# Products of a pair of heads in a fixed order, whole and one at a time

## The chip, the core and the metric

The kernel runs on one core of one Trainium2 chip. Its time is the device time of one launch in microseconds. The engines are named as in the profile: PE is TensorE (matmuls), PEld its weight loads, DVE is VectorE, ACT is ScalarE, POOL is GpSimd, SP is SyncE, which here only issues DMAs.

## The reference, cut to what matters

One decoder block on x of 512 tokens and width 2048, in float32. The part that the change touches projects x to the queries and to the gate of each head of the first attention:

```python
proj = h @ w_in[l]
(qa, kca, vca, ksa, vsa, kwa, vwa, za, ga,
 qb, kb, vb, zb) = jnp.split(proj, offsets, axis=-1)
qa = _rope(_heads(qa, N_HEADS_A, HEAD_DIM_A)).reshape(B, S, N_KV_A, GROUP_A, HEAD_DIM_A)
...
o_a = gates[..., 0:1] * o_cmp + gates[..., 1:2] * o_sel + gates[..., 2:3] * o_win
y_a = o_a.reshape(B, S, WIDTH_A) * jax.nn.silu(za)
```

There are eight heads of 128 (qa, za). After them come sixteen heads of 64 (qb, kb, vb, zb) with a sliding window, then the product with w_out, the residual and a final RMSNorm.

## The kernel before, in words

Every float32 operand of a matmul is split into two words, high and low, and a product takes three matmuls: high by high, low of one by high of the other, and high by low (`mm3`, L121 to L124). ACT makes the high word of a weight unit (128 x 1024) with a copy (L634), DVE the low word with a subtraction (L635). The pools hold three buffers for each word, so a unit that is split must wait until the third product before it has read its words.

The stage of interest is the loop over heads 1 to 7 of the first attention (L736 to L766). `pair(h)` projects the queries and the gate of one head together: the matrix of x and that of the weights are cut into quarters, and seven products of 128 x 256 outputs (Strassen's scheme in Winograd's form) replace eight. Each product is `prod` (L661): 8 x 3 = 24 matmuls with 256 moving columns each. They bear the names of their operands from x: "22", "p", "21", "12", "w", "u" and "q" in the order of the program. In the profile their lines are L122 to L124 with the tile pj; the operand is pu for "p" and "u", xh and xl for "22", "21", "12" and "w", and VH, VL, KH, KL for "q", which lies in buffers that are no longer needed for the second group of keys and values.

A head's four quarters of weights are loaded by SP into raw buffers (L671), raw0 to raw3, as x1 (quarter 3), x2 (quarter 0), x4 (quarter 2) and x3 (quarter 1). DVE forms the sums of quarters that the scheme needs in place (L684): x2 + x4, then x4 + x1, x2 + x1 and x2 + x3. The list `tags` says which buffer serves which quarter of the next head. The results of the products are combined into d and jj, by ACT copies (L700, L706, L712) and DVE additions (L684).

`attn_a(h)` (L534) is the attention of one head. For each of four blocks of 128 queries it makes a score tile (L557, tile sp, 3, 6, 6 and 9 matmuls), for which there is one PSUM buffer of three banks; DVE reduces it to minima while it scales it (L559, L563), ACT takes the exponentials (L569, L573) and scales them (L583, L585); PE transposes the weights (L595, L607, L609, tile tp), ACT and DVE split these again (L525, L526, L613 to L615), and PE multiplies with the values (L601 to L603, L616, L618, tile op).

The order in which the engines get their instructions is not written out by hand: a scheduler with a model of time picks, among instructions that are ready, and each engine then works its queue in that order. `tc.issue_after(x)` tells the scheduler to place an instruction behind x. In the kernel before, nothing binds the products of a pair to each other, so the scheduler may put matmuls of one product between those of another, and matmuls of attention of the head before between those of either.

After head 7 the even parts of x that the products' operands had replaced are loaded back (L642), two rope tables are loaded (L778, L779), and the second attention begins with the projection of its keys from two units of weights that were loaded ahead (L758 to L760). The buffers of these two units, and the counter `raws` from which later units take theirs, are set by hand.

Of the kernel before, what the change touches and what calls it, by code (L numbers as in the profile page):

```python
# [35 lines left out]
def hybrid_block(ctx, tc, xT, xtm, w0, w1s, w2s, wz, wq, wkb, wo0, wos, cw1, cw2, cpos, rope, tabs, sinks, gT, fg, out):  # L36
# [34 lines left out]
    last = {}  # L71

    raws = [0]

    def weights(tag):
        return (wk if tag == "raw3" else wp).tile([P, 1024], F32, name="raw", tag=tag, bufs=1)
# [5 lines left out]
    def words(place):  # L82
        return [wp.tile([P, 1088], F32R, name=nm, tag=nm)[:, place:place + 1024] for nm in ("whi", "wlo")]
# [35 lines left out]
    recent = {}  # L119

    def mm3(ps, ah, al, bh, bl, first, last, go_on=False):  # L121
        pe.matmul(ps, ah, bh, start=first, stop=False, skip_group_check=go_on)  # L122
        pe.matmul(ps, ah, bl, start=False, stop=False, skip_group_check=go_on)  # L123
        recent["mm"] = pe.matmul(ps, al, bh, start=False, stop=last, skip_group_check=go_on).ins  # L124
# [145 lines left out]
    H0, H1 = slice(0, 256), slice(256, 512)  # L270
# [115 lines left out]
    for g in range(2):  # L386
        act.activation(KH[g][:, 0:CMP], kct[:, g * 32:g * 32 + 32], AF.Copy)
        dve.tensor_tensor(out=KL[g][:, 0:CMP], in0=kct[:, g * 32:g * 32 + 32], in1=KH[g][:, 0:CMP].bitcast(F32),
                          op=ALU.subtract)
# [16 lines left out]
    def proj(src, parity=None, jobs=None, loaded=()):  # L406
        ps = psp.tile([P, S], F32, name="pj", tag="pj")
        ready = []
        ks = list(range(KT))
        if parity is not None:  # L410
            ks = list(range(parity, KT, 2)) + list(range(1 - parity, KT, 2))
        for i, k in enumerate(ks):
            while len(ready) < (2 if jobs or parity is not None or k >= 8 else 1):
                ready.append(load_unit(src[:, len(ready)], 1024,
                                       loaded=loaded[len(ready)] if loaded else None))
            if jobs and i in jobs:
                jobs[i]()
            hi, lo = ready[k // 8]
            js = slice((k % 8) * P, (k % 8) * P + P)
            mm3(ps, hi[:, js], lo[:, js], xh[:, k, :], xl[:, k, :], i == 0, i == KT - 1)  # L420
        return ps
# [42 lines left out]
    def z_evac(ps):  # L464
        zr = wk.tile([P, S], F32, name="zr", tag="t2", bufs=1)
        st = wk.tile([P, S], F32, name="st", tag="st")
        dve.tensor_tensor(out=zr, in0=ps, in1=rstdb, op=ALU.mult)
        act.activation(st, zr, AF.Tanh, scale=0.5)
        dve.scalar_tensor_tensor(out=st, in0=st, scalar=1.0, in1=zr, op0=ALU.add, op1=ALU.mult)
        return st  # L470
# [9 lines left out]
    def q_evac(ps, cos, sin):  # L480
        return q_split(q_rope(ps, cos, sin))

    def q_split(t1):
        qh = wk.tile([P, S], F32R, name="qh", tag="qh", bufs=1)
        ql = wk.tile([P, S], F32R, name="ql", tag="ql", bufs=1)
        act.activation(qh, t1, AF.Copy)
        dve.tensor_tensor(out=ql, in0=t1, in1=qh.bitcast(F32), op=ALU.subtract)
        return qh, ql
# [144 lines left out]
    def split(hi, lo, src):  # L633
        act.activation(hi, src, AF.Copy)  # L634
        last["lo"] = dve.tensor_tensor(out=lo, in0=src, in1=hi.bitcast(F32), op=ALU.subtract).ins  # L635
# [20 lines left out]
    def unit(raw):  # L656
        hi, lo = words(STILL)
        split(hi, lo, raw)
        return hi, lo

    def prod(bank, u, op, new):  # L661
        for m in range(8):
            cs = slice(m * P, m * P + P)
            ah, al = xf[op, m]
            mm3(bank, u[0][:, cs], u[1][:, cs], ah, al, new and m == 0, m == 7, not new)

    tags = ["raw0", "raw1", "raw2", "raw3"]

    def load_quarter(src, tag, quarter):
        t = weights(tag)  # L670
        last["dma"] = nc.sync.dma_start(t, src[quarter]).ins  # L671
        return t

    def pair(h, *early):
        src = wq[h - FIRST]
        early = list(early)
        c1, c2, c4, c3 = tags
        tags[:] = c4, c1, c3, c2

        def load(tag, quarter):  # L680
            return early.pop(0) if early else load_quarter(src, tag, quarter)

        def plus(out, a, b, op=ALU.add):
            return dve.tensor_tensor(out=out, in0=a, in1=b, op=op).ins  # L684

        pa, pb = [psp.tile([P, S], F32, name="pj", tag="pj") for e in range(2)]
        qv = wk.tile([P, S], F32, name="t1", tag="t1", bufs=1)
        zr = wk.tile([P, S], F32, name="zr", tag="xr", bufs=1)
        d, jj = qv[:, H1], zr[:, H0]
        x1 = load(c1, 3)  # L690
        u0 = unit(x1)
        x2 = load(c2, 0)
        u3 = unit(x2)
        x4 = load(c4, 2)
        with ExitStack() as behind:
            if "jj" in last:
                behind.enter_context(tc.issue_after(last["jj"]))
            plus(x2, x2, x4)
        prod(pb[:, H0], u0, "22", True)
        act.activation(d, pb[:, H0], AF.Copy, scale=-1.0)  # L700
        x3 = load(c3, 1)
        prod(pa[:, H0], u3, "p", True)
        plus(d, d, pa[:, H0])
        u2 = unit(x3)
        prod(pb[:, H0], u2, "21", False)
        act.activation(zr[:, H1], pb[:, H0], AF.Copy)  # L706
        plus(jj, d, zr[:, H1])
        u4 = unit(x2)
        plus(x4, x4, x1)
        plus(x2, x2, x1)  # L710
        prod(pa[:, H0], u4, "12", False)
        act.activation(qv[:, H0], pa[:, H0], AF.Copy)  # L712
        plus(jj, jj, qv[:, H0], ALU.subtract)
        u1 = unit(x4)
        prod(pa[:, H1], u1, "w", True)
        plus(d, d, pa[:, H1])
        u5 = unit(x2)
        plus(x2, x2, x3)
        prod(pb[:, H1], u5, "u", True)
        plus(d, d, pb[:, H1])  # L720
        t2 = wk.tile([P, S], F32, name="t2", tag="t2", bufs=1)
        for a, b in ((0, 64), (64, 0)):
            dve.tensor_tensor(out=t2[a:a + 64], in0=qv[b:b + 64], in1=sinA[b:b + 64], op=ALU.mult)
        dve.tensor_tensor(out=qv, in0=qv, in1=cosA, op=ALU.mult)
        dve.tensor_tensor(out=qv, in0=qv, in1=t2, op=ALU.add)
        qq = q_split(qv)
        u6 = unit(x2)
        prod(pb[:, H1], u6, "q", False)
        plus(jj, jj, pb[:, H1])
        last["jj"] = plus(zr, zr, rstdb, ALU.mult)  # L730
        st = wk.tile([P, S], F32, name="st", tag="st")
        act.activation(st, zr, AF.Tanh, scale=0.5)
        dve.scalar_tensor_tensor(out=st, in0=st, scalar=1.0, in1=zr, op0=ALU.add, op1=ALU.mult)
        return qq, st

    for h in range(8):  # L736
        if h < FIRST:
            qq = q_evac(q0, cosA, sinA)
            st = z_evac(proj(wz[8], 0))
            lows, highs = slice(0, 4), slice(4, 8)  # L740
            first = []
            with tc.issue_after(last["dma"]):
                first.append(load_quarter(wq[0], tags[0], 3))
                forms_back(0, lows)
                forms_back(1, lows)
            for c, quarter in zip(tags[1:], (0, 2, 1)):
                with tc.issue_after(last["dma"]):
                    first.append(load_quarter(wq[0], c, quarter))
            with tc.issue_after(last["dma"]):
                for f in (2, 3):  # L750
                    forms_back(f, lows)
                    forms_back(f, highs)
        else:
            qq, st = pair(h, *first) if h == FIRST else pair(h)
        if h == 7:
            early = []
            for u in range(2):
                early.append(weights(("raw3", "raw1")[u]))  # L758
                with tc.issue_after(last["dma"]):
                    last["dma"] = nc.sync.dma_start(early[u], wkb[:, u]).ins  # L760
        attn_a(h, *qq, st)
        if h == 3:
            for e in range(2):
                nc.sync.dma_start((KH, KL)[e][0].bitcast(F32), Kd[e])
            for e in range(2):
                nc.sync.dma_start((VH, VL)[e][:, 0].rearrange("p t w c -> p (t w c)").bitcast(F32), Vd[e])  # L766
# [133 lines left out]
        finish(8 + i, ob, st)  # L900

    kb1 = wk.tile([P, S], F32, name="kb1", tag="xr", bufs=1)
    raws[0] += 1
    q_rope(proj(wkb, parity=1, loaded=early), cosB, sinB, kb1)
    q2 = qb_evac(proj(wz[16]), 0)
    build_k(kb1, 0)
# [179 lines left out]
    for n in range(1, 4):  # L1086
# [51 lines left out]
        def plus(out, a, b, op=ALU.add):  # L1138
            dve.tensor_tensor(out=out, in0=a, in1=b, op=op)
# [52 lines left out]
        else:  # L1192
# [64 lines left out]
            u1 = [pair()]  # L1257
# [122 lines left out]
```

## Time and profile before

| | us |
|---|---|
| runs (3): median, lowest, highest | 820.22, 819.86, 821.95 |
| the profiled execution: time, span | 820.54, 818.8 |
| busy in the span: PE, DVE, ACT, POOL | 805.6, 666.6, 483.6, 67.7 |
| stage of heads 1 to 7 (196 to 401): PE, DVE busy of 205 | 203.17, 187.60 |

The profile is of one execution, whose own time stands beside its span. A matmul is recorded as busy from its start to a modelled end, and the next one starts before that end, so a start-to-start distance is the better measure of PE's pace; idle time in brackets behind a row is what is left after the modelled end of the one before, and after the arrow stands who ended it.

### The profile page before, as it was taken

How to read it: one execution, taken by the hardware profiler on the slowest of the kernel's cores; microseconds unless marked ns; L12 is line 12 of the kernel's file. 1: busy time of each engine (PE TensorE's matmuls, PEld its weight loads, DVE VectorE, ACT ScalarE, POOL GpSimd, SP SyncE). 2: the span in 40 equal slices, each digit the busy share in tenths (PEclk: the TensorE clock that was granted, in tenths of full speed). 3: DMA queues.
4: the chain of work that ended last, by engine and by line, in shares of the span. 5: the costliest groups of instructions: out<-in, count | busy, mean ns of one | idle time of the engine just before them, and what ended most of it. 6: DMA issues, size and time to landing. Idle time of an engine off the chain costs nothing.

```text
span 818.8 us, 14134 instructions
## 1 busy us (share of the span) xinstructions
PE 805.6 (98%) x5281; PEld 733.7 (90%) x5281; DVE 666.6 (81%) x1326; ACT 483.6 (59%) x1026; POOL 67.7 (8%) x54
## 2 busy tenths in 40 slices
PE   9999999999999999999999999999999999999996
PEld 8888898999999999999988888888888888999996
DVE  7859786966889899899876688887687799777895
ACT  6734456564867687786756365645444657543545
POOL 4500002020000000000011211011001000000000
PEclk9999999999999999999999999999999999999999
DMA  9665786898421322423742422222222257497845
GB/s 327 201 204 168 264 289 226 258 333 306 137 85 33 116 78 93 168 83 99 233 141 68 138 78 55 75 87 69 78 78 77 77 145 260 145 244 205 242 99 205
DMA packets 52116, 128.30 MB, mean 157 GB/s; under 512 B 4944, under 2 KB 17232, under 8 KB 52048
## 3 DMA queue, kind: packets, MB, share of 16 engines
q1 hardware_dynamic: 50032, 120.59, 43.9%
q0 software_dynamic: 1728, 6.29, 4.4%
q8 instruction: 41, 0.67, 0.3%
q10 hardware_dynamic: 288, 0.52, 0.2%
q14 instruction: 27, 0.22, 0.1%
HBM read 110.31 MB, written 17.07 MB: 156 GB/s over the span
## 4 chain that ended last, share of the span: by engine, by line
PE 85%; DVE 5%; DMA 4%; ACT 3%; issue 2%; POOL 1%; SPq 0%; DVEq 0%; ACTq 0%; POOLq 0%
PE pj L124 16%; PE pj L123 16%; PE pj L122 16%; PE bank L124 4%; PE bank L122 4%; PE oa L123 4%; PE bank L123 4%; PE oa L122 4%; PE oa L124 3%; PE sp L557 3%; DMA rw<-wos 2%; PE tp L595 2%; PE tp L879 2%; DMA xr<-xT 1%; PE spb L844 1%
## 5 line engine op out<-in xcount | busy, mean ns | idle before, releaser
L124 PE MATMUL pj<-xh,wlo 128*128 128x512 f32 (+1 forms) x560 | 194.9, 348 | 1.8 <-DVE wlo L635 1.8
L122 PE MATMUL pj<-xh,whi 128*128 128x512 f32 (+1 forms) x560 | 194.7, 348 | 0.0
L123 PE MATMUL pj<-xl,whi 128*128 128x512 f32 (+1 forms) x560 | 194.6, 347 | 0.0
L96 DVE TENSOR_TENSOR wlo<-raw,whi 128x1024 fp32r<-128x1024 f32 (+2 forms) x102 | 116.7, 1148 | 34.8 <-ACT whi L95 29.4
L95 ACT ACTIVATE whi<-raw 128x1024 fp32r<-128x1024 f32 (+1 forms) x101 | 95.0, 943 | 76.9 <-PE pj L123 22.8
L124 PEld LDWEIGHTS pj<-xh,wlo 128*128 128x128 f32 x560 | 105.4, 188 | 15.0 <-DVE wlo L635 2.4
L123 PEld LDWEIGHTS pj<-xl,whi 128*128 128x128 f32 x560 | 105.3, 188 | 13.1 <-issue 0.9
L122 PEld LDWEIGHTS pj<-xh,whi 128*128 128x128 f32 x560 | 105.3, 188 | 12.2
L635 DVE TENSOR_TENSOR wlo<-raw,whi 128x1024 fp32r<-128x1024 f32 x49 | 59.5, 1220 | 9.3 <-ACT whi L634 9.2
L634 ACT ACTIVATE whi<-raw 128x1024 fp32r<-128x1024 f32 x49 | 51.1, 1054 | 21.1 <-DVE raw L684 6.1
L123 PE MATMUL oa<-wlo,yh 128*128 128x256 f32 (+1 forms) x168 | 50.2, 299 | 0.1
L122 PE MATMUL oa<-whi,yh 128*128 128x256 f32 (+1 forms) x168 | 49.8, 298 | 0.6 <-ACT yh L954 0.6
L124 PE MATMUL oa<-whi,yl 128*128 128x256 f32 (+1 forms) x168 | 49.5, 298 | 0.0
L858 ACT ACTIVATE ttb<-ttb,sums 128x256 f32<-128x256 f32 (+1 forms) x64 | 30.1, 471 | 26.5 <-DVE sums L851 26.1
L525 ACT ACTIVATE ph<-tp 128x512 fp32r<-128x512 f32 x56 | 32.4, 592 | 14.9 <-PE tp L595 8.7
L123 PE MATMUL bank<-wlo,xh 128*128 128x256 f32 (+1 forms) x128 | 40.3, 317 | 0.3 <-DVE wlo L96 0.3
L124 PE MATMUL bank<-whi,xl 128*128 128x256 f32 (+1 forms) x128 | 39.9, 314 | 0.0
L526 DVE TENSOR_TENSOR pl<-tp,ph 128x512 fp32r<-128x512 f32 x56 | 37.8, 684 | 1.9 <-ACT ph L525 1.8
L122 PE MATMUL bank<-whi,xh 128*128 128x256 f32 (+1 forms) x128 | 36.7, 318 | 1.5 <-ACT whi L95 1.5
L122 PE MATMUL bank<-xh,whi 128*128 128x512 f32 x96 | 37.3, 400 | 0.0
L123 PE MATMUL bank<-xl,whi 128*128 128x512 f32 x96 | 36.9, 389 | 0.0
L573 ACT ACTIVATE tt<-tt,sums 128x128 f32<-128x128 f32 (+3 forms) x64 | 35.3, 554 | 1.2 <-DVE sums L563 1.2
(359 smaller groups left out, 2172.6 us busy)
## 6 DMA issues: line engine op xcount, KB each, us to landing
raw<-wz SPq DMA_DIRECT2D x36, 512.0 KB, 3.6
raw<-wq SPq DMA_DIRECT2D x28, 512.0 KB, 3.7
raw<-cw SPq DMA_DIRECT2D x16, 512.0 KB, 4.6
raw<-wos SPq DMA_DIRECT2D x12, 512.0 KB, 4.6
rw<-wos SPq DMA_DIRECT2D x10, 512.0 KB, 5.6
xr<-xT SPq DMA_DIRECT2D x16, 256.0 KB, 5.0
raw<-w SPq DMA_DIRECT2D x8, 512.0 KB, 4.5
fd<-ft SPq DMA_DIRECT2D x4, 1024.0 KB, 6.2
```

The lines of the kernel that those rows point to most:

```text
L95: last["hi"] = act.activation(hi[:, :width], rw[:, :width], AF.Copy).ins
L96: last["lo"] = dve.tensor_tensor(out=lo[:, :width], in0=rw[:, :width], in1=hi[:, :width].bitcast(F32), op=ALU.subtract).ins
L122: pe.matmul(ps, ah, bh, start=first, stop=False, skip_group_check=go_on)
L123: pe.matmul(ps, ah, bl, start=False, stop=False, skip_group_check=go_on)
L124: recent["mm"] = pe.matmul(ps, al, bh, start=False, stop=last, skip_group_check=go_on).ins
L525: act.activation(ph, tp, AF.Copy)
L526: dve.tensor_tensor(out=pl, in0=tp, in1=ph.bitcast(F32), op=ALU.subtract)
L557: pe.matmul(sp[:, a:b], qq[:, qs], kk[0][:, ko:ko + b - a], start=pi == 0, stop=pi == 2)
L573: act.activation(tv, tv, AF.Exp, bias=mn[:, i, 1 + w:2 + w], scale=-1.0, accum_out=dn[:, i, 1 + w:2 + w])
L634: act.activation(hi, src, AF.Copy)
L635: last["lo"] = dve.tensor_tensor(out=lo, in0=src, in1=hi.bitcast(F32), op=ALU.subtract).ins
L858: act.activation(tv, tv, AF.Exp, bias=mn[:, e, v:v + 1], scale=-1.0, accum_out=dn[:, e, v:v + 1])
```

## The change

Each product but "q" is recorded in `last["prod"]` by its last matmul, and the first matmul of every product of a pair is to be issued behind that one. "u" comes before "w" in the program, and with it unit u5 before u1; the addition x4 + x1 comes after "12". The buffers of the next head follow: its quarters x1, x2, x4 and x3 take the buffers that x1, x3, x4 and x2 had. The two early key units move to raw0 and raw3, and the counter of raw buffers goes on by two.

```diff
         for m in range(8):
             cs = slice(m * P, m * P + P)
             ah, al = xf[op, m]
-            mm3(bank, u[0][:, cs], u[1][:, cs], ah, al, new and m == 0, m == 7, not new)
+            with ExitStack() as behind:
+                if m == 0 and "prod" in last:
+                    behind.enter_context(tc.issue_after(last["prod"]))
+                mm3(bank, u[0][:, cs], u[1][:, cs], ah, al, new and m == 0, m == 7, not new)
+        if op != "q":
+            last["prod"] = recent["mm"]
...
         c1, c2, c4, c3 = tags
-        tags[:] = c4, c1, c3, c2
+        tags[:] = c1, c3, c4, c2
...
         u4 = unit(x2)
-        plus(x4, x4, x1)
         plus(x2, x2, x1)
         prod(pa[:, H0], u4, "12", False)
         act.activation(qv[:, H0], pa[:, H0], AF.Copy)
         plus(jj, jj, qv[:, H0], ALU.subtract)
-        u1 = unit(x4)
-        prod(pa[:, H1], u1, "w", True)
-        plus(d, d, pa[:, H1])
+        plus(x4, x4, x1)
         u5 = unit(x2)
         plus(x2, x2, x3)
         prod(pb[:, H1], u5, "u", True)
         plus(d, d, pb[:, H1])
+        u1 = unit(x4)
+        prod(pa[:, H1], u1, "w", True)
+        plus(d, d, pa[:, H1])
...
-                early.append(weights(("raw3", "raw1")[u]))
+                early.append(weights(("raw0", "raw3")[u]))
...
     kb1 = wk.tile([P, S], F32, name="kb1", tag="xr", bufs=1)
-    raws[0] += 1
+    raws[0] += 2
```

## The prediction

> **What bounds the kernel now.** I read the page first, then the busy times by stretch over the stage that the change touches (heads 1 to 7 of the first attention, 196 to 401 us), then who waited for whom there, then PE's timeline around each wait.
>
> ```profile
> span 818.8 us, 14134 instructions
> PE 805.6 (98%) x5281; PEld 733.7 (90%) x5281; DVE 666.6 (81%) x1326; ACT 483.6 (59%) x1026; POOL 67.7 (8%) x54
> PE 85%; DVE 5%; DMA 4%; ACT 3%; issue 2%; POOL 1%; SPq 0%; DVEq 0%; ACTq 0%; POOLq 0%
> ```
>
> ```profile
> 196.00:227.00 31.00, 30.68 (x249) 29.84 (x249) 28.35 (x64) 22.33 (x51) 0.00 (x0) 1.00 0.57 196
> 257.00:288.00 31.00, 31.00 (x255) 30.21 (x256) 28.47 (x63) 22.32 (x58) 0.00 (x0) 1.00 0.24 77
> 318.00:349.00 31.00, 30.04 (x251) 29.35 (x250) 27.43 (x62) 21.88 (x56) 0.00 (x0) 1.00 0.33 111
> sum 205.00, PE 203.17 PEld 198.59 DVE 187.60 ACT 152.11 POOL 0.00; mean PE 29.02 PEld 28.37 DVE 26.80 ACT 21.73 POOL 0.00
> ```
>
> PE is the bound. The last four lines are three of the seven stretches, one for each head, and their sum: PE is busy 203.17 of 205.00 us at a granted clock of 1.00, so its visible idle time in the whole stage is 1.83 us. DVE is second with 187.60, 92%, and it works in order, so it can hold PE up only where something that PE needs stands late in DVE's queue. Where that happens:
>
> ```profile
> PE pj L124 <- DVE wlo L635: 1.8, 3, 1.0
> ```
>
> ```profile
> 220.69 0.39 PE L124 MATMUL pj<-xh,wlo 128*128 128x256 f32 x1 [0.32 <-DVE wlo L635]
> 250.40 0.28 PE L123 MATMUL pj<-xl,whi 128*128 128x256 f32 x1
> 251.19 0.39 PE L124 MATMUL pj<-xh,wlo 128*128 128x256 f32 x1 [0.52 <-DVE wlo L635]
> 339.89 0.28 PE L123 MATMUL pj<-xl,whi 128*128 128x256 f32 x1
> 341.12 0.39 PE L124 MATMUL pj<-xh,wlo 128*128 128x256 f32 x1 [0.96 <-DVE wlo L635]
> ```
>
> Three waits are all there is. Each is the first matmul with the low word in the first product ("22") of the next head, after both matmuls that need only the high word. Why the low word is late shows in what PE did before the last of them:
>
> ```profile
> 331.02 0.28 PE L123 MATMUL pj<-pu,whi 128*128 128x256 f32 x1
> 332.22 0.28 PE L124 MATMUL pj<-pu,wlo 128*128 128x256 f32 x1
> 333.70 0.28 PE L122 MATMUL pj<-pu,whi 128*128 128x256 f32 x1
> 333.81 0.28 PE L122 MATMUL pj<-xh,whi 128*128 128x256 f32 x1
> ```
>
> Product "u" (operand pu) starts at 330.8, is broken off at 333.81 for the whole of "w" (operand xh), and ends only near 338.8. So its sum into d, and the weight words that it holds (three buffers for each word), come free late, and DVE meets the next head's split behind a score reduction. Such nesting is what the change forbids.
>
> **The change part by part.** *Order of the products.* Nothing is added or removed: the built order of the changed kernel has the same 5218 matmuls, and DVE's queue the same operations. Each product of a pair begins after the last matmul of the one before, and w comes after u. Attention may still cut in, and does: counted along PE's queue, the 49 products of the stage stand in 109 pieces before and in 107 after. What must go are nested products, and with them the causes of the three waits. From start to start the two large ones cost 341.12 - 339.89 - 0.11 = 1.12 and 251.19 - 250.40 - 0.11 = 0.68 us; with 0.32 for the small one that is 2.1 us. In the new order "q" is over before "22" of the next head begins, and DVE has that low word 1 to 4 us ahead of PE at all six borders between heads. What is late next is the chain of score tiles.
>
> That chain: the scores have one PSUM buffer (sp), so each of a head's four tiles waits until DVE has reduced the tile before, and DVE does it behind whatever stands ahead. Before, PE could fill such a time with a second product. To walk along the new order I need these prices:
>
> ```profile
> 293.14 0.18 DVE L559 CUSTOM_DVE_ANT_0 tc__3271<-sp,tab 128x32 f32<-128x32 f32 x1
> 293.94 2.35 DVE L635 TENSOR_TENSOR wlo<-raw,whi 128x1024 fp32r<-128x1024 f32 x2
> 385.07 2.35 DVE L635 TENSOR_TENSOR wlo<-raw,whi 128x1024 fp32r<-128x1024 f32 x2
> 387.34 1.28 DVE L526 TENSOR_TENSOR pl<-tp,ph 128x512 fp32r<-128x512 f32 x2
> 388.54 1.21 DVE L684 TENSOR_TENSOR raw<-raw 128x1024 f32<-128x1024 f32 x1
> 338.51 0.19 DVE L559 CUSTOM_DVE_ANT_0 tc__3674<-sp,tab 128x32 f32<-128x32 f32 x1 [1.36 <-PE sp L557]
> 339.85 1.22 DVE L635 TENSOR_TENSOR wlo<-raw,whi 128x1024 fp32r<-128x1024 f32 x1
> ```
>
> ```profile
> 262.03 0.74 PE sp L557 x6
> 295.35 1.08 PE sp L557 x6
> ```
>
> ```profile
> L634 ACT ACTIVATE whi<-raw 128x1024 fp32r<-128x1024 f32 x49 | 51.1, 1054 | 21.1 <-DVE raw L684 6.1
> raw<-wq SPq DMA_DIRECT2D x28, 512.0 KB, 3.7
> ```
>
> By starts, a split on DVE takes (387.34 - 385.07) / 2 = 1.14 us, and so does an addition of weights; a split of transposed scores 0.60; the reduction of the second score tile 293.94 - 293.14 = 0.80, of the fourth 339.85 - 338.51 = 1.34. The second and third tile take PE 0.74 and 1.08.
>
> The walk through head 4, from the end of "21" as zero. PE: "12" 24 x 0.117 = 2.8; two transposes 0.2; second score tile 0.74, to 3.75; six transposes 0.65, to 4.4; two matmuls of "u", to 4.65; then the third tile, which waits for the reduction of the second: DVE begins it at about 3.9 and ends it at 4.7, so PE loses 0.1 to 0.2. Third tile to 5.9. Next is u's first low word: DVE's split follows the reduction, 4.7 + 1.14 = 5.85, just in time. Later PE needs the buffer for the first tile of head 4's own scores at 26.1: DVE has reduced the fourth tile of head 3 at 26.1 to 26.3, and then come pcr and ql, each 0.1 behind PE. So 0.5 us for this head. Heads 5 and 7 show the same two places: about 0.4 (ql and pcr again), and about 0.2 (the first tile's reduction stands behind two splits and an addition, 3.4 us, while PE arrives after seven matmuls of "u"). Heads 1 to 3 and 6 have margins of 1 to 5 us everywhere; I put 0.3 for what the walk doesn't see. Sum of the added: 1.4 us. Its bounds are 0 (each place is a margin of 0.1 to 0.3, and half the steps may be quicker) and the largest wait of the trace in each of seven heads, 7 x 0.96 = 6.7; I take 1.4 because it comes from the order itself.
>
> *Pitch.* PE streams these products in two paces, in each of which it stays for a product or more:
>
> ```profile
> 283.81 0.28 PE L122 MATMUL pj<-VH,whi 128*128 128x256 f32 x1
> 286.52 0.28 PE L124 MATMUL pj<-KH,wlo 128*128 128x256 f32 x1
> 301.32 0.28 PE L122 MATMUL pj<-xh,whi 128*128 128x256 f32 x1
> 303.92 0.28 PE L124 MATMUL pj<-xh,wlo 128*128 128x256 f32 x1
> ```
>
> Both pairs of rows are the first and last of 24: 2.71 / 23 = 117.8 ns and 2.60 / 23 = 113.0 ns. Along the timeline 22 of the 49 products have a median of 117 or 118, 27 of 113 to 115. A product that changes pace moves the end by 24 x 4.8 ns = 0.115 us, so -2.5 (all quick) to +3.1 (all slow). The pace follows no operation of another engine that I could find, and the number of cuts by attention stays (109 and 107), so I take 0, with a likely spread of 11 products, 1.3 us, either way. The Trainium skill ("TensorE: Matmul & The Clock Gate", section "Back-to-back issue gap") gives N / 2.4 + 2.5 ns for a lone matmul, 109 ns here; neither pace reaches it, and at 109 in all 1176 matmuls the time would be some 8 us shorter.
>
> *Weight sums and buffers.* x4 + x1 moves behind "12", u's unit ahead of w's: the same 1.14 us each on a queue with 8% to spare, in the walk already. x1, x3, x4, x2 are now dead in that order; each load of the next head is issued on SP when its buffer's last reader is done, lands 3.7 us later and is read some 10 us after that. Cover gone, a late load would cost its 3.7 us once; I see none.
>
> *The first key units.* They move to other buffers and the parity of the following ones with them; SP now issues the first unit of the next projection between the two key halves, since its buffer is free sooner. Behind them on SP stand the four reloads of x and the two rope tables:
>
> ```profile
> xh<-xd SPq DMA_DIRECT2D x2, 512.0 KB, 7.0
> 413.15 0.69 DVE L780 TENSOR_TENSOR cosA<-cosA,rstdb 128x512 f32<-128x512 f32 x1 [2.15 <-DMA cosA<-rope]
> ```
>
> The reloads wait for the last "w", which is now later in the head; from its end to the first matmul that reads them lie "q", two score and value groups and 24 matmuls of the projection, about 13 us against 7.0. DVE's wait of 2.15 for the table cost PE nothing, as the long matmuls covered it; the table is asked for earlier now. I put 0.
>
> The sum: 820.54 (the profiled execution, span 818.8) - 2.1 + 1.4 = 819.8. That execution lies 0.3 above the median of the runs, 820.22, so the forecast for the median is 819.5.
>
> **The rivals.** *The score chain binds (slower).* PE's queue is in order: at 341.12 everything behind one matmul stood still for 0.96 us. With no second product to fill, each head could pay one such wait, at the third tile or at the next head's first. For it: the walk has margins of only 0.1 at five places. Against: DVE has 17 us of slack in the stage. It decides if DVE comes to these reductions over 0.6 us later than I walked. Time: 819.5 - 1.4 + 6.7 = 824.8. The Trainium skill speaks for it: the same page, section "Architectural detail: the array is 16× 32×32, not 1× 128×128", says that PE's window pulls weight loads ahead of running matmuls, and that is all it reorders; the wait at 341.12 agrees.
>
> *More than the waits goes (faster).* No nested product holds buffers, the walk's margins all hold, and half of the slow products turn quick: 819.5 - 1.4 - 1.3 = 816.8. For it: a free run of products settles in the quick pace (301.32 to 303.92). Against: the pace also stays slow through whole uncut products (283.81 to 286.52).
>
> *All the pace turns slow (slower).* 819.5 + 3.1 = 822.6, on the border of what can be told.
>
> *It does not do what it says.* The wish is on order alone, and the built queue shows it fulfilled, so I give it no chance.
>
> **How the numbers follow.** 0.3%, about what a measurement of this kernel can tell from no change, is 2.5 us: faster means below 817.8, slower above 822.7. Within it, the forecast: 0.43, as the gain and the price are both near 2. Score chain or pace against it: 0.30 (0.24 and 0.06), since every error of a walk by hand adds waits. Faster: 0.27. The range runs from the faster rival, 816.8, to the score chain in every head, 824.8; the likeliest case alone has 817.8 to 822.
>
> **What would show it.** Right: in the stage no wait of the first "22" of a head for wlo; new short ones of L557 on DVE, or of L595 and L616 on its splits, 1 to 2 us together; PE idle near 1 us; 49 products of which about half at 113 ns; nothing new behind 402 us. Wrong: PE idle above 4 us with L557 named, or a mean pitch that moved by over 1.5 ns, or a wait for a DMA in the stage or at the key projection.

## The result and the profile after

| kernel | median us | runs | ratio to the kernel before, 95% interval |
|---|---|---|---|
| before (same runs) | 820.65 | 6 | |
| changed | 825.00 (824.24 to 826.42) | 6 | 1.0056 [1.0045, 1.0066] |

Slower by 4.4 us, where 819.5 was forecast, and 0.2 us above the range. The profiled execution took 824.74 us. Its page, in the lines that were read before (busy time of each engine; the chain that ended last, by engine; dots stand for what is left out):

```profile
span 823.0 us, 14144 instructions
...
PE 807.0 (98%) x5281; PEld 735.1 (89%) x5281; DVE 665.7 (81%) x1326; ACT 485.0 (59%) x1026; POOL 66.9 (8%) x54
...
PE 81%; DVE 6%; DMA 5%; ACT 4%; issue 2%; POOL 1%; SPq 0%; ACTq 0%; DVEq 0%; POOLq 0%
```

The work is the same and DVE is no busier; the chain has moved from PE to DMA, DVE and ACT. The busy times by stretch over the stage (length, then PE, PEld, DVE, ACT and POOL, then PE's granted clock, DMA share and GB/s):

```profile
288.00:318.00 30.00, 28.68 (x240) 28.04 (x239) 27.05 (x61) 21.87 (x54) 0.00 (x0) 1.00 0.37 116
...
379.00:401.00 22.00, 19.40 (x148) 18.57 (x147) 15.64 (x40) 15.13 (x39) 0.00 (x0) 0.92 0.62 200
sum 205.00, PE 200.40 PEld 196.34 DVE 183.43 ACT 148.18 POOL 0.00; mean PE 28.63 PEld 28.05 DVE 26.20 ACT 21.17 POOL 0.00
```

PE now stands still for 205.00 - 200.40 = 4.60 us in the same 205 us, against 1.83 before: 2.8 us more. The last stretch holds 2.60 of it, and there, and only there, the granted clock is below 1. Who waited for whom in the stage (us in total, times, longest), all of PE, and of ACT the row that matters:

```profile
PE tp L595 <- ACT tt L585: 2.6, 2, 1.9
PE sp L557 <- DMA KH<-Kd: 1.2, 1, 1.2
PE pj L122 <- ACT t L705: 0.5, 2, 0.3
```

```profile
ACT st L737 <- DMA yd<-st: 8.2, 4, 5.4
```

The three waits for wlo are gone, as forecast. No wait of L557 for DVE is named either. What is new is a wait of ACT for the store of a head's result, four times. ACT's timeline around the longest:

```profile
377.60 0.38 ACT L705 ACTIVATE t<-pj 128x256 f32<-128x256 f32 x1
383.42 0.63 ACT L737 ACTIVATE st<-zr 128x512 f32<-128x512 f32 x1 [5.44 <-DMA yd<-st]
383.95 1.99 ACT L634 ACTIVATE whi<-raw 128x1024 fp32r<-128x1024 f32 x2
385.85 0.68 ACT L583 ACTIVATE pc<-tc__4073,sums 128x128 f32<-128x128 f32 x2
386.43 2.33 ACT L585 ACTIVATE tt<-tt,sums 128x384 f32<-128x384 f32 x4
```

L737 is the tanh of a head's gate, written to st. st has two buffers, so head 6 needs that of head 4, which `finish` (L498) fills with head 4's result and SP stores to yd. Here is the instruction that fills it, and what SP issued around it:

```profile
377.71 0.68 DVE L498 SCALAR_TENSOR_TENSOR st<-op,st 128x512 f32<-128x512 f32 x1
```

```profile
376.29 2.15 SPq L505 DMA_DIRECT2D yp<-yd  x4
378.55 0.38 SPq L500 DMA_DIRECT2D yd<-st  x1
```

The store was issued at 378.55 and landed 4.8 us later, and only then could the tanh start. Four reloads of earlier results, 256 KB each (yp<-yd), stood ahead of it on SP. The other three stores whose landing a tanh awaited took 2.0 us (issued at 282.90, with nothing just ahead of it), 4.4 (313.67, behind the reload of K) and 2.8 (344.32, behind that of V). Nobody needs the tanh soon. But ACT works in order, and behind it stood two weight splits, pc and the scalings tt, for which PE's transposes waited:

```profile
384.88 0.28 PE L124 MATMUL pj<-xh,wlo 128*128 128x256 f32 x1
387.09 0.44 PE L595 MATMUL tp<-ident,tt 128*128 128x128 f32 x2 [1.92 <-ACT tt L585]
388.20 1.11 PE L595 MATMUL tp<-ident,tt 128*128 128x128 f32 x6 [0.68 <-ACT tt L585]
...
389.46 0.41 PE L123 MATMUL pj<-pu,whi 128*128 128x256 f32 x1
389.68 0.41 PE L124 MATMUL pj<-pu,wlo 128*128 128x256 f32 x1
...
392.63 0.28 PE L123 MATMUL pj<-pu,whi 128*128 128x256 f32 x1
392.75 0.29 PE L124 MATMUL pj<-pu,wlo 128*128 128x256 f32 x1
```

Behind the stall the matmuls stand 0.22 us apart (389.46 to 389.68), not 0.12 as at 392.63. The stretches say why (clock in the third number from the end):

```profile
389.00:392.00 3.00, 3.00 (x15) 2.93 (x15) 2.13 (x5) 3.00 (x11) 0.00 (x0) 0.51 0.85 281
392.00:392.50 0.50, 0.50 (x4) 0.50 (x3) 0.16 (x3) 0.28 (x1) 0.00 (x0) 0.53 0.19 74
```

Half the clock for 3.4 us costs 0.49 x 3.0 + 0.47 x 0.5 = 1.7 us, on top of the stall, while PE counts as busy. With the 2.8 us of added idle time that makes 4.5 us; the spans differ by 4.2. The slow clock is not peculiar to the profiled execution: the mean granted clock is 0.994 to 0.996 in all six runs of the changed kernel, and 0.997 or more in 65 of the 76 runs of the kernel before that were timed beside the experiments.

### The profile page after: what moved, and what is told of

Its sections match the earlier page's. It is cut to its first block, busy times and chain, and to the rows that moved or that the text cites. A ratio compares the mean times of both kernels' runs of the same rounds, so it can differ in the third digit from the quotient of the medians.

```text
span 823.0 us, 14144 instructions
## 1 busy us (share of the span) xinstructions
PE 807.0 (98%) x5281; PEld 735.1 (89%) x5281; DVE 665.7 (81%) x1326; ACT 485.0 (59%) x1026; POOL 66.9 (8%) x54
## 4 chain that ended last, share of the span: by engine, by line
PE 81%; DVE 6%; DMA 5%; ACT 4%; issue 2%; POOL 1%; SPq 0%; ACTq 0%; DVEq 0%; POOLq 0%
PE pj L122 15%; PE pj L123 15%; PE pj L124 15%; PE bank L124 4%; PE bank L122 4%; PE oa L123 4%; PE oa L122 4%; PE oa L124 4%; PE bank L123 3%; PE sp L557 3%; DMA rw<-wos 2%; PE tp L595 2%; PE tp L884 2%; DMA xr<-xT 1%; DMA raw<-cw 1%
## 5 line engine op out<-in xcount | busy, mean ns | idle before, releaser
L573 ACT ACTIVATE tt<-tt,sums 128x128 f32<-128x128 f32 (+3 forms) x64 | 35.3, 554 | 1.2 <-DVE sums L563 1.2
```

Of the source, the lines that this page charges most:

```text
L573: act.activation(tv, tv, AF.Exp, bias=mn[:, i, 1 + w:2 + w], scale=-1.0, accum_out=dn[:, i, 1 + w:2 + w])
```

## The experiments

Theory D, after the traces: the loss is waits for transfers, the store ahead of the tanh and, at 317.5 us, the reload of K. Rival O: the fixed order itself costs the time. Rival B: the new order of the weight buffers does. All runs were timed in five rounds beside the kernel before, whose medians in the three groups were 820.93, 820.66 and 820.56 us.

### Taking the store off the buffer

```diff
-        dve.scalar_tensor_tensor(out=dst, in0=op, ...)
+        done = dve.scalar_tensor_tensor(out=dst, in0=op, ...).ins
         if h < 8:
-            nc.sync.dma_start(yd[h], st)
+            with tc.issue_after(done):
+                nc.sync.dma_start(yd[h], cosA)
```

> The changed kernel, but the store of a head's result (heads 0 to 7) reads the cosine table instead of st, and is issued after the same instruction as before: the results of these heads are left out of the output; the transfers keep their number and size, but no buffer of st waits for a store. Theory D (the loss is waits for transfers: the tanh L737 of a head waits for the store of the head two before, about 5 us at 383 us, and the first score tile of head 4 for the reload of K, about 1.9 us at 317 us): 820 to 822 us, and the idle time of ACT before the tanh that ends with the store, 8.2 us in the changed kernel, is gone. Rival O (the fixed order itself delays the score chain or the products, whatever the buffers): 824.5 to 826. Rival B (the other order of the weight buffers costs it): 824.5 to 826.

Measured: 818.76 us (7 runs), 0.9973 [0.9963, 0.9984] of the kernel before: 6.2 us less than the changed kernel, faster than before, and below the range expected. The one wait of PE that is left in the stage:

```profile
PE sp L558 <- ACT tt L574: 0.7, 1, 0.7
```

One dependence, with all transfers still made, is worth more than the whole loss of 4.4 us. O and B fall as explanations of it.

The control for it is the same edit of the kernel before:

> Control for the first run: the kernel before, with the store of a head's result (heads 0 to 7) reading the cosine table instead of st; the results of these heads are left out. Theory D: no tanh waits for a store in the kernel before, so nothing changes: 820 to 821.5 us. If the stores slowed the kernel in another way: 815 to 819 us, and the gain of the first run (6.2 us) says less of the tanh.

Measured: 820.70 us (11 runs), 1.0007 [0.9996, 1.0019]. In the kernel before no tanh waits for a store: the results of heads 1 to 5 are ready 10 to 19 us ahead of the tanh that takes their buffer, as in these two rows of its timeline,

```profile
366.51 0.69 DVE L498 SCALAR_TENSOR_TENSOR st<-op,st 128x512 f32<-128x512 f32 x1 [0.93 <-PE op L618]
```

```profile
381.52 0.62 ACT L732 ACTIVATE st<-zr 128x512 f32<-128x512 f32 x1
```

against 2.7 to 5.7 us for four heads of the changed kernel, their waits included (377.71 and 383.42). The gain of the first run is the tanh's wait and not the stores.

### A third buffer of st

```diff
-            pd = wk.tile([P, 256], F32, name="pd", tag="pd", bufs=1)
-            pcr = wk.tile([P, 256], F32R, name="pcr", tag="pcr", bufs=1)
+            pd = wk.tile([P, S], F32, name="pd", tag="pl")[:, 0:256]
+            pcr = wk.tile([P, S], F32R, name="pcr", tag="ph")[:, 0:256]
...
-                pd = wk.tile([P, 256], F32, name="pd", tag="pd", bufs=1)
+                pd = wb.tile([P, 256], F32, name="pd", tag="pd")
```

> Control for the next: the changed kernel with the tiles pd and pcr put into buffers of pl and ph (pd of the second half of the heads into a pool of its own), which frees the room for a third buffer of st, and nothing more. All theories: 824.5 to 826 us, that is within 1.5 us of the changed kernel; a larger shift would be the price of the moved tiles and is to be taken off the next.

Measured: 823.78 us (6 runs), 1.0040 [1.0026, 1.0054], 0.7 us below the range expected. The wait for the store is there as before (8.4 us in four), and so is PE's stall, a little shorter:

```profile
388.35 0.44 PE L595 MATMUL tp<-ident,tt 128*128 128x128 f32 x2 [1.63 <-ACT tt L585]
389.47 1.05 PE L595 MATMUL tp<-ident,tt 128*128 128x128 f32 x6 [0.68 <-ACT tt L585]
...
390.57 0.28 PE L123 MATMUL pj<-pu,whi 128*128 128x256 f32 x1
390.68 0.28 PE L124 MATMUL pj<-pu,wlo 128*128 128x256 f32 x1
```

After 1.63 instead of 1.92 us the clock is not halved in this execution (0.11 us from 390.57 to 390.68). Whether that makes the 1.2 us by which this control is faster is not shown: the mean clock of three of its six runs is 0.995 or 0.996, as in the changed kernel.

The next run adds the buffer, at both places where st is made (one is shown):

```diff
-        st = wk.tile([P, S], F32, name="st", tag="st")
+        st = wk.tile([P, S], F32, name="st", tag="st", bufs=3)
```

> The kernel of the control with three buffers of st in place of two. Theory D: 3 to 5 us less than the control, 820 to 822 us, with no wait of the tanh for a store; the wait of the first score tile of head 4 for K stays. Rivals O and B: as the control, 824.5 to 826.

Measured: 821.33 us (11 runs), 1.0011 [0.9999, 1.0022], 2.5 us below the control; no wait for a store is left. One more buffer removes the same wait as the first run did, so this half of D holds. 3 to 5 us had been expected; the control's stall, 1.63 + 0.68 us without a slow clock in the profiled execution, may have had less to give. The kernel stays 2.6 us above that of the first run, which lost the same waits; why is not settled.

### The reload of K

```diff
-                nc.sync.dma_start((KH, KL)[e][0].bitcast(F32), Kd[e])
+                nc.sync.dma_start((KH, KL)[e][0][:, :800].bitcast(F32), Kd[e, :, :800])
+                nc.sync.dma_start((KH, KL)[e][0][:, 800:].bitcast(F32), Kd[e, :, 800:])
```

> As the one before, and K's words of the second group are reloaded in two pieces each, the first 800 columns ahead of the rest, so that the first score tile waits for a shorter transfer. Theory D: another 0.5 to 2 us less, 818.5 to 821 us, below the kernel before, since the three waits for wlo (2.1 us) stay gone. Rivals O and B: 824.5 to 826.

Measured: 821.35 us (12 runs), 1.0009 [0.9996, 1.0021]; nothing gained. The edit did not do what it was meant to: SP got KL's second piece ahead of KH's first. KH was issued at 316.68, where the run with three buffers alone had 314.11, but this profiled execution, at 825.17 us the slowest of the twelve, was already 2.9 us late there (the reduction that frees sp ended at 321.5 against 318.6), so KH was issued neither earlier nor later. So once more, with the order of the four pieces fixed and the first of 288 columns:

```diff
-            for e in range(2):
-                nc.sync.dma_start((KH, KL)[e][0].bitcast(F32), Kd[e])
+            with ExitStack() as behind:
+                for cs in (slice(0, 288), slice(288, CMP + 1024)):
+                    for e in range(2):
+                        behind.enter_context(tc.issue_after(
+                            nc.sync.dma_start((KH, KL)[e][0][:, cs].bitcast(F32), Kd[e, :, cs]).ins))
```

> The kernel with three buffers of st, and the reload of K in two pieces, KH ahead of KL and the first 288 columns ahead of the rest, so that the first score tile of head 4 waits for a piece of 144 KB (the run with 800 columns first had KL's second piece ahead of KH's first on the queue, and KH was issued no earlier). Theory D (the reload is what that tile waits for): 1 to 1.5 us less than with three buffers alone, the gap ahead of the first score tile of head 4 from 1.4 us to below 0.4 us. Rival C (the chain of splits and exponentials on DVE and ACT ends at the same time): the gap stays above 1 us and the time within 0.5 us.

Measured: 820.84 us (11 runs), 1.0004 [0.9995, 1.0013], 0.5 us below the run with three buffers, and the gap stays. KH's first piece was issued at 312.95 and landed 2.2 us later. The last reduction of head 3's fourth score tile on DVE, and PE's first score tile of head 4:

```profile
317.11 0.68 DVE L563 CUSTOM_DVE_ANT_0 tt<-sp,tab 128x512 f32<-128x512 f32 x1
317.72 0.08 DVE L563 DVE_READ_ACCUMULATOR2_ANT sums<- 128x1 f32 x1
```

```profile
318.06 0.37 PE L557 MATMUL sp<-KH,qh 128*128 128x288 f32 x1 [1.13 <-ACT tt L573]
```

The tile starts 0.3 us behind the reduction that frees the single buffer sp, and 2.9 us behind the landing. (The profile names the exponentials on ACT, L573, which ended at about the same time; the kernel has sp read by DVE alone.) The other half of D falls. In the changed kernel the reduction was over at 316.7 and the reload landed at 317.4, so at most 0.7 us there was the transfer's; the rest is the score chain.

### Which part of the change does it

The change has three parts: the fixed order, u before w, and the buffers that follow. (The place of the addition x4 + x1 goes with u before w in every run below; it was not run by itself.) First the order alone, on the kernel before:

```diff
+            with ExitStack() as behind:
+                if m == 0 and "prod" in last:
+                    behind.enter_context(tc.issue_after(last["prod"]))
...
+        if op != "q":
+            last["prod"] = recent["mm"]
```

> The kernel before with the fixed order of the products alone (each product issued after the one before it); u before w in issue, the order of the weight buffers and the early key units stay those of before. What is asked is which part of the change puts the stores close to the tanh. Theory D1 (the order alone does it: the products go ahead of the attention, the results of a head come some 5 to 12 us later, and the tanh waits for a store): 822 to 826 us, idle time of ACT at the tanh that ends with a store of 4 us or more. Theory D2 (it takes the other sequence of u and w or the other buffers as well): 818.5 to 821 us, no such wait; the three waits for wlo (1.8 us) gone.

Then the changed kernel without the order, and with the old buffers:

```diff
-        tags[:] = c1, c3, c4, c2
+        tags[:] = c4, c1, c3, c2
...
-                early.append(weights(("raw0", "raw3")[u]))
+                early.append(weights(("raw3", "raw1")[u]))
...
-    raws[0] += 2
+    raws[0] += 1
```

> The changed kernel without the fixed order: w after u in the text, the weight buffers and the early key units as changed. Theory D1: 819.5 to 822 us, near the kernel before, no wait of the tanh for a store above 1 us. Theory D2: 822 to 826 us if the sequence and the buffers alone do it.

> The changed kernel with the weight buffers and the early key units in the order of before; the fixed order and u before w stay. Theory D1: 823 to 826 us, the wait of the tanh for the store as in the changed kernel (4 us or more at the sixth tanh). Theory B (the other order of the buffers is what costs): 819 to 821.5 us.

And u before w taken back in the changed kernel (shown), or made alone, the opposite edit, in the kernel before:

```diff
...
+        u1 = unit(x4)
+        prod(pa[:, H1], u1, "w", True)
+        plus(d, d, pa[:, H1])
         u5 = unit(x2)
         plus(x2, x2, x3)
         prod(pb[:, H1], u5, "u", True)
         plus(d, d, pb[:, H1])
-        u1 = unit(x4)
-        prod(pa[:, H1], u1, "w", True)
-        plus(d, d, pa[:, H1])
```

> The changed kernel with w issued before u again; the fixed order and the new order of the weight buffers stay. Theory S (it is u before w that draws the splits of u and w together ahead of the score reading on DVE, so that the attention of a head ends 8 to 12 us later and its store meets the tanh): 815.5 to 818.5 us, the result of a head (L498) 10 us or more ahead of the tanh of the head after next, no wait for a store. Rival B (the order of the buffers costs 2.6 us by itself, the difference between the changed kernel and the run with the old buffers): 818.5 to 820.5 us.

> The kernel before with u issued before w alone: no fixed order, the buffers as before. Theory S: the attention is late here too, the tanh waits for a store: 821.5 to 825 us. Rival (u before w hurts only together with the fixed order, which was what gave 5.9 us between the order alone and the order with u first): 819.5 to 821.5 us, the waits for wlo as before.

| fixed order | u before w | new buffers | median us | ratio to before | idle of ACT at the tanh until a store |
|---|---|---|---|---|---|
| no | no | no | (before) | 1 | none |
| yes | no | no | 816.53 | 0.9951 [0.9935, 0.9966] | none |
| yes | no | yes | 816.28 | 0.9954 [0.9941, 0.9968] | none |
| no | yes | no | 825.41 | 1.0070 [1.0051, 1.0088] | 6.6, 2 times |
| no | yes | yes | 822.37 | 1.0023 [1.0010, 1.0035] | 2.9, 2 times |
| yes | yes | no | 822.42 | 1.0024 [1.0011, 1.0036] | 3.2, 2 times |
| yes | yes | yes | 825.00 | 1.0056 [1.0045, 1.0066] | 8.2, 4 times |

The new buffers alone, the eighth combination, were not run. The rows part cleanly. w first: no wait for a store, and the order gains 4 us against the kernel before, with either set of buffers. u first: slower than before in every row. My theory that the order alone pushes the stores late is wrong, and B is too. Of the times expected, 816.28 came, and 822.37 as D2 had it, 0.4 us past D1; 816.53 lies below both theories, 825.41 lies 0.4 us above its range, and 822.42 between those of B and D1. The buffers move the time by 3 us one way without the order and 2.6 us the other with it, only where u is first and so where the tanh meets the store; why by so much in each row is not settled. By the same rows the order, where u is first, gains 3.0 us with the old buffers and costs 2.6 with the new. The store is not the only transfer that is awaited there: in the stage ACT also waits 1.3 to 4.8 us for loads of weights (raw<-wq) in each row with u first, and in none with w first.

What u first does stands in DVE's timeline. The reduction of a score tile is L559 (minima of the compressed part) and twice L563. The third tile of head 3, in the changed kernel:

```profile
298.07 0.18 DVE L559 CUSTOM_DVE_ANT_0 tc__3271<-sp,tab 128x32 f32<-128x32 f32 x1
...
300.11 1.22 DVE L635 TENSOR_TENSOR wlo<-raw,whi 128x1024 fp32r<-128x1024 f32 x1
...
301.35 1.18 DVE L635 TENSOR_TENSOR wlo<-raw,whi 128x1024 fp32r<-128x1024 f32 x1
...
303.75 1.22 DVE L635 TENSOR_TENSOR wlo<-raw,whi 128x1024 fp32r<-128x1024 f32 x1 [0.82 <-ACT whi L634]
...
306.41 0.56 DVE L563 CUSTOM_DVE_ANT_0 tt<-sp,tab 128x384 f32<-128x384 f32 x1
...
315.29 0.18 DVE L559 CUSTOM_DVE_ANT_0 tc__3271<-sp,tab 128x32 f32<-128x32 f32 x1
```

And with w first again, order and new buffers kept:

```profile
299.70 0.19 DVE L559 CUSTOM_DVE_ANT_0 tc__3271<-sp,tab 128x32 f32<-128x32 f32 x1
...
299.82 0.55 DVE L563 CUSTOM_DVE_ANT_0 tt<-sp,tab 128x384 f32<-128x384 f32 x1
...
305.34 0.19 DVE L559 CUSTOM_DVE_ANT_0 tc__3271<-sp,tab 128x32 f32<-128x32 f32 x1 [1.22 <-PE sp L557]
```

In the changed kernel three splits for the following products stand inside the reduction of one tile. sp stays taken for 9 us, PE streams the rest of "u", all of "w" and "q" and nearly all of the next pair's "22" before the fourth tile (92 matmuls, against 31 with w first; no gap over 0.25 us), and the fourth tile is reduced at 315.29, 17.2 us behind the third; with w first it is 5.6 us. The head's result is late by that, and its store moves up to the tanh two heads on. In the seven orders of the table the results of heads 1 to 5 come 10 to 20 us ahead of that tanh where w is first and 3 to 11 us where u is. What tears the reduction was not tried. The splits need not be the cause: L563 writes tt, whose one buffer for this half the transposes of the head before still read. In the changed kernel the last of these (L607) ran at 303.15, in the midst of the torn reduction; with w first at 297.36, before the third tile. In head 2 L563 waits for one of them by name (0.67 us at 272.85).

The kernel with w first has the stage that the prediction described (its page, the sum of the stretches over 196 to 401 us, PE's waits):

```profile
span 814.7 us, 14146 instructions
...
PE 93%; DMA 2%; DVE 2%; ACT 1%; issue 1%; POOL 0%; SPq 0%; DVEq 0%; ACTq 0%
```

```profile
sum 205.00, PE 204.27 PEld 201.28 DVE 189.36 ACT 155.97 POOL 0.00; mean PE 29.18 PEld 28.75 DVE 27.05 ACT 22.28 POOL 0.00
```

```profile
PE sp L557 <- DVE sums L563: 0.5, 1, 0.5
PE pj L122 <- DVE zr L689: 0.3, 1, 0.3
```

At 816.28 us it is the fastest kernel of this study, with the order alone (816.53), from which its interval does not part it. With u first alone the waits of PE are others, and behind the longer of them the clock is halved again:

```profile
320.47 0.58 PE L557 MATMUL sp<-KH,qh 128*128 128x288 f32 x1 [2.66 <-DVE st L498]
```

```profile
320.50:323.00 2.50, 2.50 (x11) 2.50 (x12) 2.41 (x5) 0.68 (x1) 0.00 (x0) 0.50 0.76 151
```

### Moving the tanh instead

```diff
-                act.activation(tv, tv, AF.Copy, scale=...)
+                last["tt"] = act.activation(tv, tv, AF.Copy, scale=...).ins
...
-        act.activation(st, zr, AF.Tanh, scale=0.5)
+        with tc.issue_after(last["tt"]):
+            act.activation(st, zr, AF.Tanh, scale=0.5)
```

> The changed kernel with two buffers of st as it has, and the tanh of a head issued after the last scaling (tt, L585) of the attention of the head before, which stands 3 to 8 us behind it on ACT. Theory D: what waited behind the tanh (two halves of weights, the scalings) goes ahead, the store lands meanwhile: 819.5 to 822 us, idle time at the tanh below 1 us. Rival L (the tanh is then late for the next head, whose copy into zr has to wait for it): 823 to 827 us, with ACT or PE waiting for zr.

Measured: 819.06 us (12 runs), 0.9980 [0.9970, 0.9991], 5.9 us below the changed kernel. u is still first and the fourth tiles are still late (reduced at 311.4, third 299.9), yet no tanh waits for a store; PE's waits in the stage are 1.1 us in three:

```profile
381.57 2.34 ACT L585 ACTIVATE tt<-tt,sums 128x384 f32<-128x384 f32 x4
383.81 0.61 ACT L738 ACTIVATE st<-zr 128x512 f32<-128x512 f32 x1
```

So most of the price of the lateness falls due when an instruction that must wait for the store stands ahead of work that PE needs. It is not free without that: this kernel and that of the first run, 818.76, stay 2.8 and 2.5 us above the one with w first, of which PE's idle time in the stage explains 0.6 and 0.3 us (busy 203.68 and 203.95 against 204.27). The rest is open.

## Why the prediction was wrong

- **The waits for wlo, -2.1 us: right.** They are gone in every kernel with the fixed order, and the order alone gives -4.1 us, -4.3 with the new buffers. (They are gone too in both kernels with u first and no order, so the order is not the only cure.) PE's idle time in the stage falls by 1.1 us (1.83 to 0.73), and the waits counted from start to start were 2.1; the other 2 us were not traced. With w first the time is that of the rival "more than the waits goes", 816.8, but not by its turn of pace: 20 of the 49 products are slow there, against 22 before.
- **The added, +1.4 us: the step that failed.** The walk priced a late reduction of a score tile only where PE next needs sp. It even met the late fourth tile (head 3's, at 26.1 to 26.3 of its walk) and charged 0.1 us. It did not follow the head to its end: result, store, buffer of st, tanh, and what is queued behind the tanh on ACT. That chain measured 6.2 us by the first run: in the longest case the stall of 1.92 + 0.68 us and 1.7 us of slow clock. Of the 8.7 us between u first and w first (825.00 and 816.28) it leaves 2.5 open.
- **Transfers in the stage, 0: wrong.** "Weight sums and buffers" looked at the loads of weights and saw none late; one was, by 1.7 us for ACT at 302.66, and PE did not wait. The stores of results and the reload of K were not looked at. The store had 10 to 19 us of cover before and 2.7 to 5.7 after, their waits included; its landing, 2.0 to 4.8 us and longest behind reloads, was then in the open.
- **The slow clock: not in the sum at all.** All stretches of before showed 1.00, and no term allowed for a stall to change that.
- **The change taken as a whole.** The prediction spoke of "the change" as the order, and put u before w among moves "in the walk already". The runs show that the order is worth -4.1 and u before w +4.8 by itself (825.41). (Its 5218 matmuls stand in no profile; the pages count 5281, before and after.)
- **Pitch, 0: right.** By the same count as before, 19 of the 49 products are slow, against 22.
- **Key units and tables, 0: right** with w first, where new buffers move the time from 816.53 to 816.28; with u first it can't be told apart from the store's wait.
- **The rival of the score chain, 824.8 at 0.24:** nearly the right time by another mechanism. The chain was late by far more than the 0.6 us named, but PE, which had other products to run, did not wait for it; ACT did, for the store. Only the 1.2 us at 317.5 went as that rival said. The last paragraph of the prediction named the sign that came: PE idle above 4 us, and a wait for a DMA in the stage.

## What to carry to other kernels

When a change makes one chain later, follow that chain to its last instruction, a store included, and to whoever needs the buffer that the store frees; then look at what is queued behind that one on an in-order engine. Compare each store's distance from the next write of its buffer with its landing time, in both orders and with what stands ahead of it on the queue, for it is not in any busy time. And where a change has several parts, run each alone: here a gain of 4 us was hidden under a loss of nearly 9.

## What was not expected of the hardware

In the changed kernel PE's clock fell to 0.50 after idle times of 1.92 and 0.68 us, with eight transposes and no other matmul from 385.16 to 389.08, and stayed there for 3.4 us. With u first alone it fell in the course of a single idle time of 2.66 us. The control with the small tiles had 1.63 and 0.68 us, and 3.6 us with transposes alone, and stayed at 1.00. The length of the idle time does not decide by itself: in the profiled execution of the first run on K the clock fell twice, after 1.11 and 0.39 us and after 1.35 us, while with three buffers alone the same wait of 1.26 us did nothing.

```profile
128.17 0.38 PE L236 MATMUL bank<-whi,F 128*128 128x256 f32 x1 [1.11 <-ACT whi L95]
...
321.76 0.37 PE L557 MATMUL sp<-KH,qh 128*128 128x288 f32 x1 [1.35 <-ACT tt L573]
```

```profile
130.00:132.00 2.00, 2.00 (x10) 1.98 (x9) 0.36 (x2) 2.00 (x5) 1.62 (x2) 0.50 0.79 256
...
324.00:326.00 2.00, 2.00 (x12) 2.00 (x11) 1.76 (x4) 0.42 (x1) 0.00 (x0) 0.50 0.00 0
```

So a stall of 1.3 or 1.4 us can cost 1.7 us more, or nothing. Runs of one kernel differ with it: of the 76 runs of the kernel before, the 11 with a mean clock of 0.995 or 0.996 took 822.2 us on average, the other 65 took 820.6. The Trainium skill ("TensorE: Matmul & The Clock Gate", section "Part 1: The HAM clock gate (the "warmup" mystery)") says that idling takes the clock from full to half and no step between, and the 0.50 and 0.51 here agree. It says that this takes an idle window of about 3.4 us, and a busy one of that length to return; the return took 3.4 us here too, but the idle times ahead of the falls were shorter.
